# Moving a bank subtraction and a norm's sum behind the first group's sums on VectorE, in a matmul with RMSNorm

## The chip, the cores and the metric

The kernel runs on one core of one Trainium2 chip. The metric is the device time of one execution in microseconds (us). The program gives each engine its own list of instructions: TensorE (PE in the profile) multiplies, PEld is its weight load, VectorE is DVE, ScalarE is ACT, GpSimd is POOL, SyncE is SP. This kernel's matmuls write into eight banks of the memory called PSUM; a bank can be given to a new product only when the last reader of the old one is done with it.

## The reference

```python
# a: 2048x2048, b: 2048x2048, gamma: 2048, all float32; eps = 1e-5
x = np.matmul(a, b)
rms = np.sqrt(np.mean(x ** 2, axis=-1, keepdims=True) + eps)
return gamma * x / rms
```

## The kernel before

A is cut into 16 blocks of 128 rows. Blocks 0 to 3 are the "head". The others are worked in "groups" of two blocks, group 2 (blocks 4 and 5) first. Within a group, each half of the columns is computed by seven products (of eight matmuls each) rather than eight, at the price of sums: VectorE makes the sums s1, s2, s5, s6, s7 of quarters of the transposed A, and it and ScalarE combine the seven results. (In the code below, `...` marks what was cut, and the comments are added.)

```python
def take_transposed(mb, g, view, copy):            # half a transposed block: PSUM -> at(mb)
    copy(out=at(mb)[:, g * 8:(g + 1) * 8, :], in_=view)

def row_norm(mb):                                  # ScalarE: norm of a row of A, for scaling to fp16
    ... # two Squares with an accumulator (L219), then:
    nc.scalar.activation(out=norm[mb], in_=n2[:, 0:1], func=ACTF.Sqrt, ...)          # L222

def row_factor(mb):                                # VectorE: needs norm[mb]
    ...
    nc.vector.tensor_scalar_max(out=s, in0=norm.pop(mb), scalar1=1e-18)              # L227
    ...

def a_sums(g, which, lo=0, hi=KP):                 # VectorE: s1, s2, ... of a group       L260
    a11, a12, a21, a22 = (quarter(g, r, c) for r in range(2) for c in range(2))
    terms = {1: (a11, a22, ALU.add), 2: (a21, a22, ALU.add), 5: (a11, a12, ALU.add), ...}
    ...

def take_rms(mb):                                  # the norm of a row of the output
    ...
    nc.vector.reduce_sum(out=tot, in_=msq.pop(mb), axis=...)                         # L335
    ...
    nc.scalar.activation(out=rms_of[mb], in_=tot, func=ACTF.Sqrt)                    # L337
```

The boundary between the head and the groups; the change is made here:

```python
p6 = new_bank()
product(PAIR, 1, 6, p6)                            # TensorE: last product of the head
a_sums(G0, (5,))                                   # needs block 4 only
nc.vector.tensor_tensor(out=x22, in0=pair[1], in1=x22, op=ALU.subtract)   # L551, reads a bank
for g in range(2):
    turn(HB + 1, g)                                # TensorE transposes half of block 5
    take_transposed(HB + 1, g, turned[HB + 1, g], nc.vector.tensor_copy)  # L192
square_half(0, 1)
square_half(1, 1)
take_rms(0)
a_sums(G0, (2, 1))                                 # need block 5
```

The first half of group 2 (j=0), written out in order of issue (`p2`, `p5` and the others are PSUM banks; seven rotate in a pool, and the eighth, `tbank`, last served a transpose). A hook is work of other blocks that is put between the products:

```python
# hook 0: finish(0, (1,))
product(g, j, 5, p5)                               # group 2, j=0: product 5 is first
nc.scalar.copy(out=c, in_=p5)                      # L591
# hook 1: row_norm(6); take_rms(1)
product(g, j, 2, p2)
nc.vector.tensor_tensor(out=t, in0=p2, in1=c, op=ALU.add)                 # L595
# hook 2: row_factor(6); finish(0, (0,)); row_apply(6); row_norm(7); a_sums(2, (7, 6));
#         finish(1); row_factor(7); pair_sums(); pair_ends()
product(g, j, 1, p1)
nc.vector.tensor_tensor(out=t, in0=p1, in1=t, op=ALU.subtract)            # L599
product(g, j, 4, p2, start=False)                  # accumulates into p2: waits for L595
...                                                # products 3, 7, 6; then j=1: 2, 5, 1, 4, 3, 7, 6

def pair_ends():
    nc.vector.tensor_tensor(out=x11, in0=p7, in1=x11, op=ALU.add)   # L565: frees the head's p7 bank
    nc.vector.tensor_tensor(out=x22, in0=p6, in1=x22, op=ALU.add)   # L566
```

In the built program, p5 of the second half (j=1) of group 2 is given the PSUM bank that L565 frees. That is not visible in the source; it follows from the order in which banks are taken and released.

Of the kernel before, what the change touches and what calls it, by code (L numbers as in the profile page):

```python
# [13 lines left out]
ALU = mybir.AluOpType  # L14
# [3 lines left out]
def kernel(  # L18
# [13 lines left out]
    nc = tc.nc  # L32
# [12 lines left out]
    G0 = HB // 2  # L45
# [200 lines left out]
    def quarter(g, r, c):  # L246
        if g < G0:
            return head_at[:, c::2, 2 * g + r, :]
        return at(2 * g + r)[:, c::2, :]

    def sum_of(g, s):
        return s_sum[s].bitcast(BF16) if g < G0 else s_sum[s]

    def a_sums(g, which, lo=0, hi=KP):
        a11, a12, a21, a22 = (quarter(g, r, c) for r in range(2) for c in range(2))
        terms = {1: (a11, a22, ALU.add), 2: (a21, a22, ALU.add), 5: (a11, a12, ALU.add),
                 6: (a21, a11, ALU.subtract), 7: (a12, a22, ALU.subtract)}
        for s in which:
            x, y, op = terms[s]
            nc.vector.tensor_tensor(out=sum_of(g, s)[:, lo:hi, :], in0=x[:, lo:hi, :],  # L260
                                    in1=y[:, lo:hi, :], op=op)
# [44 lines left out]
    def square_half(mb, h):  # L306
        c = n_sq[mb]
        n_sq[mb] += 1
        sq = sq_pool.tile([P, 2 * CH], BF16, name="sq")
        nc.scalar.activation(out=sq, in_=x_tile(mb, h), func=ACTF.Square,  # L310
                             scale=inv_sqrt_n, accum_out=msq[mb][:, c:c + 1])

    def x_tile(mb, h):


        if (mb, h) not in x_half:
            n = n_x[0]
            n_x[0] += 1
            if n < 8:
                slot = n  # L320
            else:
                g = n // 4
                slot = ((0, 4, 1, 5), (0, 1, 4, 5))[g // 2 % 2 == 0][n % 4] + 2 * (g % 2)
            x_half[mb, h] = x_slot[slot]
        return x_half[mb, h]

    def x_chunk(mb, c):
        return x_tile(mb, c // 2)[:, (c % 2) * CH:(c % 2 + 1) * CH]
# [3 lines left out]
    def take_rms(mb):  # L332

        tot = stat_pool.tile([P, 1], FP32, name="tot")
        nc.vector.reduce_sum(out=tot, in_=msq.pop(mb), axis=mybir.AxisListType.X)  # L335
        rms_of[mb] = stat_pool.tile([P, 1], FP32, name="rms")
        nc.scalar.activation(out=rms_of[mb], in_=tot, func=ACTF.Sqrt)  # L337
# [123 lines left out]
    pair = {}  # L461
# [57 lines left out]
    x11, x12, x21, x22 = (x_chunk(r, c) for r in (r2, r3) for c in (2, 3))  # L519
# [28 lines left out]
    p6 = new_bank()  # L548
    product(PAIR, 1, 6, p6)
    a_sums(G0, (5,))  # L550
    nc.vector.tensor_tensor(out=x22, in0=pair[1], in1=x22, op=ALU.subtract)  # L551
    for g in range(2):
        turn(HB + 1, g)
        take_transposed(HB + 1, g, turned[HB + 1, g], nc.vector.tensor_copy)
    square_half(0, 1)
    square_half(1, 1)
    take_rms(0)
    a_sums(G0, (2, 1))

    def pair_sums():  # L560
        nc.vector.tensor_tensor(out=x11, in0=x22, in1=x21, op=ALU.add)
# [284 lines left out]
```

## Time and profile before

| | before |
|---|---|
| time, 3 runs | 221.41 us (221.40 to 221.79) |
| span of the profiled run | 219.9 us |
| PE busy | 209.3 us (95%) |
| VectorE, ScalarE busy | 165.9 us (75%), 127.0 us (58%) |

TensorE is the limit. Its listed waits in the kernel before are four, of which three end before 12 us; the fourth (waiter, what it waited for, us in total, times, longest us) is:

```profile
PE acc L285 <- DVE s L260: 0.5, 1, 0.5
```

That one wait, for VectorE's sums, is the last before a long unbroken run. The end of the chain of waits (start us, us, what) shows it:

```profile
68.60 0.67 DVE s L260
69.27 0.05 issue
69.32 141.76 PE acc L285 x656
```

From 69.32 us, TensorE issues 656 matmuls and waits for nothing. So time won ahead of 69.32 us is won for the whole kernel, provided that nothing inside the run becomes late. The timeline of TensorE in the kernel before (start us, us, engine, line, operation, tiles and shapes, count, and in brackets the idle time before with what ended it):

```profile
66.97 1.89 PE L285 MATMUL acc<-b,s 128*128 128x512 bf16 x8
69.32 1.90 PE L285 MATMUL acc<-b,s 128*128 128x512 bf16 x8 [0.46 <-DVE s L260]
71.06 1.89 PE L285 MATMUL acc<-t_left,s 128*128 128x512 bf16 x8
72.78 3.62 PE L285 MATMUL acc<-t_left,at_even 128*128 128x512 bf16 x16
76.24 7.07 PE L285 MATMUL acc<-b,s 128*128 128x512 bf16 x32
83.14 1.89 PE L285 MATMUL acc<-early,s 128*128 128x512 bf16 x8
...
210.92 1.91 PE L790 MATMUL acc<-b,s 128*128 128x256 bf16 x16
```

These are product 5; 2; 1; 4 and 3; 7 and 6 followed by 2 and 5 of the second half; and 1 of the second half; the last line is the two half-size products at the very end. The pitch of two matmuls is read from the starts, 3.46 us for 16, thus 0.216 us; the 0.379 us that a matmul is given in the records contains a modelled end. Product 2 could have started at 66.97 + 8 x 0.216 = 68.70 us and started at 69.32, so 0.62 us of issue time were lost, not the 0.46 us in the bracket.

VectorE at the same place (timeline, kernel before), from s5 to the instruction that frees the bank:

```profile
66.05 0.69 DVE L260 TENSOR_TENSOR s<-at_even 128x1024 f16<-128x1024 f16 x1 [0.21 <-ACT at_even L192]
66.66 0.68 DVE L551 TENSOR_TENSOR x<-acc,x 128x512 f32<-128x512 f32 x1
67.26 0.68 DVE L192 COPY at_even<-tbank 128x1024 f16<-128x1024 f16 x1
67.86 0.68 DVE L192 COPY at_even<-acc 128x1024 f16<-128x1024 f16 x1
68.46 0.14 DVE L335 TENSOR_REDUCE tot<-msq 128x1 f32<-128x5 f32 x1
68.57 1.29 DVE L260 TENSOR_TENSOR s<-at_even 128x1024 f16<-128x1024 f16 x2
...
72.07 0.15 DVE L227 TENSOR_SCALAR s<-norm 128x1 f32<-128x1 f32 x1
...
79.78 0.68 DVE L565 TENSOR_TENSOR x<-acc,x 128x512 f32<-128x512 f32 x1
```

And ScalarE (timeline, kernel before): the square root of the norm's sum, the copy behind it, and the root that ends the row norm of block 6.

```profile
68.64 0.20 ACT L337 ACTIVATE rms<-tot 128x1 f32<-128x1 f32 x1
68.89 0.59 ACT L591 COPY head_at<-acc 128x512 f32<-128x512 f32 x1
...
71.74 0.29 ACT L222 ACTIVATE norm<-n 128x1 f32<-128x1 f32 x1
```

The three views together hold what follows. The subtraction (L551) and the norm's sum (L335) stand ahead of the sum s2 for which TensorE waits. But ScalarE's root L337 starts as soon as L335 has ended, the copy L591 and the row norm up to L222 follow behind it, and VectorE's L227 starts 0.04 us after L222's end. And L565 ends at 80.46 us, while TensorE wants its bank at 83.14 - 1.73 = 81.41 us: 0.95 us of slack, about 0.9 us after the 0.05 us that a release takes to reach TensorE (s2 ended at 69.27 in the chain above, and product 2 started at 69.32).

### The profile page before, as it was taken

How to read it: one execution, taken by the hardware profiler on the slowest of the kernel's cores; microseconds unless marked ns; L12 is line 12 of the kernel's file. 1: busy time of each engine (PE TensorE's matmuls, PEld its weight loads, DVE VectorE, ACT ScalarE, POOL GpSimd, SP SyncE). 2: the span in 40 equal slices, each digit the busy share in tenths (PEclk: the TensorE clock that was granted, in tenths of full speed). 3: DMA queues.
4: the chain of work that ended last, by engine and by line, in shares of the span. 5: the costliest groups of instructions: out<-in, count | busy, mean ns of one | idle time of the engine just before them, and what ended most of it. 6: DMA issues, size and time to landing. Idle time of an engine off the chain costs nothing.

```text
span 219.9 us, 3044 instructions
## 1 busy us (share of the span) xinstructions
PE 209.3 (95%) x1032; PEld 97.4 (44%) x1032; DVE 165.9 (75%) x326; ACT 127.0 (58%) x263; POOL 36.3 (16%) x75
## 2 busy tenths in 40 slices
PE   7799999999999999999999999999999999999970
PEld 3344544444454444444444444444444444444440
DVE  1128799999889999979795639946695659787781
ACT  2110002920599898688745997289747996334471
POOL 7544443343020002100200002000200000000040
PEclk9999999999999999999999999999999999999996
DMA  7999999999929895948799049965699249145045
GB/s 157 164 203 206 199 206 208 212 206 228 409 76 362 291 293 118 358 176 230 213 300 405 3 93 265 351 247 95 156 294 405 42 100 364 73 174 210 1 171 212
DMA packets 36864, 46.60 MB, mean 212 GB/s; under 512 B 22256, under 2 KB 26352, under 8 KB 35568
## 3 DMA queue, kind: packets, MB, share of 16 engines
q0 software_dynamic: 10608, 23.86, 44.1%
q1 hardware_dynamic: 25824, 22.02, 33.5%
q10 hardware_dynamic: 416, 0.52, 0.7%
q8 instruction: 8, 0.13, 0.2%
q14 instruction: 8, 0.07, 0.1%
HBM read 34.60 MB, written 16.78 MB: 234 GB/s over the span
## 4 chain that ended last, share of the span: by engine, by line
PE 65%; DMA 23%; ACT 4%; POOL 2%; issue 1%; DVE 1%; ACTq 0%; POOLq 0%
PE acc L285 64%; DMA b<-in_b_dram 14%; DMA early<-in_a_dram 5%; DMA a<-in_a_dram 4%; ACT sq L219 2%; POOL b L102 1%; ACT at_even L192 1%; PE acc L790 1%; POOL early L106 1%; DVE s L260 1%; DVE at_even L192 0%; ACT x L729 0%; DVE x L551 0%; ACT norm L222 0%; ACT x L531 0%
## 5 line engine op out<-in xcount | busy, mean ns | idle before, releaser
L285 PE MATMUL acc<-b,s 128*128 128x512 bf16 x408 | 93.3, 379 | 0.5 <-DVE s L260 0.5
L285 PEld LDWEIGHTS <-s 128*128 128x128 f16 (+1 forms) x512 | 49.9, 98 | 60.4 <-DVE s L260 1.0
L388 PE MATMUL acc<-b,head_at 128*128 128x512 bf16 x176 | 43.2, 379 | 1.2 <-DMA b<-in_b_dram 1.2
L303 ACT ACTIVATE sq<-x 128x512 bf16<-128x512 f32 x53 | 33.4, 630 | 6.9 <-DVE x L722 3.0
L370 DVE SCALAR_TENSOR_TENSOR x<-x,r,gamma_sb 128x1024 f32<-128x1024 f32 x28 | 34.8, 1282 | 0.7
L219 ACT ACTIVATE sq<-a 128x1024 bf16<-128x1024 f32 x24 | 25.3, 1053 | 2.1 <-DMA a<-in_a_dram 1.5
L388 PEld LDWEIGHTS <-head_at 128*128 128x128 bf16 x176 | 16.9, 98 | 20.6 <-issue 1.6
L242 ACT ACTIVATE head_at<-a,s 128x2048 f16<-128x2048 f32 x10 | 20.0, 1998 | 3.3 <-DVE s L229 3.3
L102 POOL DMA_DIRECT2D b<-in_b_dram x32 | 17.2, 540 | 20.8 <-DMA b<-in_b_dram 15.0
L430 ACT COPY x<-acc 128x512 f32<-128x512 f32 x5 | 2.9, 582 | 24.7 <-PE acc L388 24.7
L285 PEld LDWEIGHTS <-head_at 128*128 128x128 f16 (+1 forms) x112 | 10.9, 98 | 13.2
L285 PE MATMUL acc<-early,head_at 128*128 128x512 bf16 x64 | 14.5, 379 | 0.0
L285 PEld LDWEIGHTS <-at_even 128*128 128x128 f16 x96 | 9.4, 98 | 11.3
L285 PE MATMUL acc<-early,s 128*128 128x512 bf16 x56 | 14.2, 379 | 0.0
L260 DVE TENSOR_TENSOR s<-head_at 128x1024 f16<-128x1024 f16 (+5 forms) x22 | 13.4, 635 | 0.1
L609 DVE TENSOR_TENSOR x<-x,x 128x512 f32<-128x512 f32 x9 | 6.2, 692 | 8.8 <-ACT x L607 8.3
L127 POOL COPY pace<-x 128x1 f32<-128x1 f32 x4 | 1.7, 413 | 66.7 <-DVE x L618 65.6
L591 ACT COPY x<-acc 128x512 f32<-128x512 f32 x9 | 5.2, 573 | 11.5 <-PE acc L285 11.5
L173 DVE COPY head_at<-tbank 128x1024 bf16<-128x1024 bf16 x7 | 4.8, 692 | 8.7 <-PE tbank L168 8.5
L285 PE MATMUL acc<-t_left,s 128*128 128x512 bf16 x48 | 11.3, 379 | 0.0
L774 POOL TENSOR_SCALAR x<-x,r 128x512 f32<-128x512 f32 x1 | 2.7, 2652 | 51.2 <-DVE r L346 51.2
L276 DVE TENSOR_TENSOR b<-b 128x1024 bf16<-128x1024 bf16 x16 | 10.8, 684 | 0.2
(113 smaller groups left out, 237.5 us busy)
## 6 DMA issues: line engine op xcount, KB each, us to landing
out_dram<-x SPq DMA_DIRECT2D x29, 512.0 KB, 3.8
a<-in_a_dram POOLq DMA_DIRECT2D x10, 1024.0 KB, 8.7
b<-in_b_dram POOLq DMA_DIRECT2D x32, 256.0 KB, 10.0
a<-in_a_dram POOLq DMA_DIRECT2D x4, 512.0 KB, 9.8
early<-in_a_dram POOLq DMA_DIRECT2D x7, 256.0 KB, 10.2
gamma_sb<-in_gamma_dram POOLq DMA_DIRECT2D x2, 512.0 KB, 8.3
out_dram<-x SPq DMA_DIRECT2D x3, 256.0 KB, 2.6
out_dram<-a SPq DMA_DIRECT2D x1, 512.0 KB, 3.3
```

The source lines that it names most:

```text
L102: nc.gpsimd.dma_start(out=raw[j][kp][:, t, :], in_=b[lo:lo + P, j * HALF:(j + 1) * HALF])
L173: nc.vector.tensor_copy(out=head_at[:, 2 * kp:2 * kp + 2, :, :], in_=view)
L219: nc.scalar.activation(out=junk, in_=a32[mb][:, h * HALF:(h + 1) * HALF], func=ACTF.Square, scale=2.0 ** -8, accum_out=n2[:, h:h + 1])
L242: nc.scalar.activation(out=a16[mb], in_=a32.pop(mb), func=ACTF.Copy, scale=factor.pop(mb))
L260: nc.vector.tensor_tensor(out=sum_of(g, s)[:, lo:hi, :], in0=x[:, lo:hi, :], in1=y[:, lo:hi, :], op=op)
L276: nc.vector.tensor_tensor(out=flat[:, 1:3, :], in0=flat[:, 1:3, :], in1=flat[:, 0::3, :], op=ALU.add)
L285: nc.tensor.matmul(bank, lhsT[:, kp, :], rhs, start=(start and kp == 0), stop=(kp == KP - 1), skip_group_check=not start)
L303: nc.scalar.activation(out=sq[:, 0:CH], in_=src, func=ACTF.Square, scale=inv_sqrt_n, accum_out=msq[mb][:, c:c + 1])
L370: nc.vector.scalar_tensor_tensor(out=x, in0=x, scalar=inverse_of[mb], in1=gamma_sb[:, h * HALF:(h + 1) * HALF], op0=ALU.mult, op1=ALU.mult)
L388: nc.tensor.matmul(bank, head_at[:, kt, r, :], head_rhs(c, kt), start=(kt == 0), stop=(kt == KT - 1))
L591: nc.scalar.copy(out=c, in_=one[1])
L609: nc.vector.tensor_tensor(out=t, in0=t, in1=x12, op=ALU.add)
```

## The change

The intent is that VectorE does first what TensorE waits for: the copies of block 5's transposes and the sums s2 and s1, then the bank's subtraction and the norm's sum.

```diff
     a_sums(G0, (5,))
-    nc.vector.tensor_tensor(out=x22, in0=pair[1], in1=x22, op=ALU.subtract)
     for g in range(2):
         turn(HB + 1, g)
         take_transposed(HB + 1, g, turned[HB + 1, g], nc.vector.tensor_copy)
     square_half(0, 1)
     square_half(1, 1)
+    a_sums(G0, (2, 1))
+    nc.vector.tensor_tensor(out=x22, in0=pair[1], in1=x22, op=ALU.subtract)
     take_rms(0)
-    a_sums(G0, (2, 1))
```

The order on the other engines is the same in the two built programs. One side effect: the banks of products 7 and 6 of group 2 are swapped, because pair[1]'s bank is released later.

## The prediction

> **What bounds it.** TensorE. The page gives PE busy for 209.3 of 219.9 us, and the chain of waits that ended last is one unbroken run of 656 matmuls from 69.32 us to the end. It starts at the boundary that this change touches: the waits give TensorE one 0.46 us wait for VectorE's first-group sums (L260). The timeline shows it: group 2's first product starts at 66.97 us; eight matmuls at a pitch of 0.216 us end at 68.70, but the second product starts only at 69.32, because its sum s2 ends at 69.26. So 0.62 us of issue time is lost there (the view counts a matmul's modelled end, hence 0.46).
>
> **What the change moves.** Nothing is added or removed; the order on the other engines is unchanged. On VectorE the bank subtraction (0.68 us, pitch 0.60) and the norm's sum (0.15) go from before s2 to behind s2 and s1.
>
> **Gain.** The first copy can start once the transposes end (66.68), at about 66.72, not 67.26; the second at 67.32; s2 at 68.05, ending 68.73; TensorE goes on at about 68.79 instead of 69.32: 0.53 us won.
>
> **Price.** The norm's sum ended at 68.60; it now ends behind s2, s1 and the subtraction, at about 70.00. ScalarE's square root waits for it (68.64 before, about 70.03 now) with everything later behind it: the Trainium skill, "PSUM — Partial Sum Buffer", section "Engine vs sequencer instructions", calls the ScalarE and VectorE queues strict FIFO, and the trace agrees (L337 at 68.64, L591 at 68.89, L219 at 69.38, back to back). So the next block's row norm ends at 73.4 instead of 72.03. VectorE reached L227, which needs that norm, at 72.02, with no slack; it now waits until about 73.46, and all behind it comes 1.39 us later:
> - s7 ends at about 76.05 (74.66 before). TensorE, 0.53 us earlier, wants it at 75.71: about 0.4 us of the gain is lost.
> - L565, which frees the head's p7 bank for p5 of the second half of group 2, ended at 80.46; TensorE wanted that bank at 81.41. It will end at about 81.85: TensorE stalls and starts that product at about 81.9, some 0.5 us later than before.
>
> After that, slack of over a microsecond at each bank and sum should absorb the shift, so the rest keeps this 0.5 us.
>
> **Predicted time.** 221.4 + 0.5 = 221.9 us, range 221.2 to 222.5 (low end: VectorE catches up; high end: another late bank, or the loads of A, which also come later). Faster by over 2%: 0.005; within 2%: 0.985; slower: 0.01.
>
> **What the profile would show.**
> 1. TensorE's s2 product starts near 68.8 (the L260 wait there is nearly gone).
> 2. ScalarE idles about 1.3 us before the square root L337, released by VectorE's L335, which starts near 69.85.
> 3. VectorE idles about 1 us before L227, released by ScalarE's L222.
> 4. TensorE waits about 0.2 us (modelled) before product 7 for L260, and about 0.5 us near 81.9 for L565.
> 5. The run of matmuls then continues without gaps, about 0.5 us later than before; the tail is unchanged.
>
> **What would make it wrong.** If the norm's delay were shorter than I think, or L227 had slack, L565 would be in time and the gain of 0.1 to 0.5 us would stay (220.9 to 221.3). If a later load or bank is also late, it is slower still. Run-to-run spread (221.40 to 221.79) is nearly as large as the effect.

## The result, and the profile after

The changed kernel took 222.10 us (median of 6 runs, 221.87 to 222.46), the kernel before 221.59 us (6 runs, 221.40 to 221.86). The ratio is 1.0023 with a 95% interval of 1.001 to 1.0036: slower by a quarter of a per cent, which by the 2% measure is the same. A ratio here is the mean time of one kernel's runs over that of the other's runs of the same rounds, so it is not quite the ratio of the medians. Executions over 1.5% slower than the fastest of the same kernel are left out of the means.

The waits of TensorE in the changed kernel no longer name the sums. In their place:

```profile
PE acc L285 <- DVE x L565: 0.5, 1, 0.5
```

The end of the chain of waits, changed kernel: the unbroken run starts later now, and behind L565.

```profile
80.54 0.69 DVE x L562
81.24 0.61 DVE x L565
81.89 129.66 PE acc L285 x600
```

TensorE's timeline, changed kernel:

```profile
67.11 3.73 PE L285 MATMUL acc<-b,s 128*128 128x512 bf16 x16
70.67 1.89 PE L285 MATMUL acc<-t_left,s 128*128 128x512 bf16 x8
72.61 3.61 PE L285 MATMUL acc<-t_left,at_even 128*128 128x512 bf16 x16
76.08 5.35 PE L285 MATMUL acc<-b,s 128*128 128x512 bf16 x24
81.89 1.89 PE L285 MATMUL acc<-b,s 128*128 128x512 bf16 x8 [0.46 <-DVE x L565]
83.61 1.89 PE L285 MATMUL acc<-early,s 128*128 128x512 bf16 x8
...
211.39 1.91 PE L790 MATMUL acc<-b,s 128*128 128x256 bf16 x16
```

Products 5 and 2 are now one stretch of 16, so the hole ahead of product 2 has all but gone: product 1 starts 3.56 us after product 5, against 3.45 us (16 pitches) without any hole and 4.09 us before. But two other holes have come. Product 4 starts at 72.61 instead of 70.67 + 1.73 = 72.40 us, and product 5 of the second half at 81.89 instead of 76.08 + 24 x 0.216 = 81.26 us. The first has no bracket, because 0.21 us is hardly more than what the modelled end hides.

VectorE, changed kernel:

```profile
66.86 0.69 DVE L192 COPY at_even<-tbank 128x1024 f16<-128x1024 f16 x1 [0.20 <-PE tbank L185]
67.47 0.68 DVE L192 COPY at_even<-acc 128x1024 f16<-128x1024 f16 x1
68.18 1.29 DVE L260 TENSOR_TENSOR s<-at_even 128x1024 f16<-128x1024 f16 x2
69.40 0.68 DVE L557 TENSOR_TENSOR x<-acc,x 128x512 f32<-128x512 f32 x1
70.00 0.15 DVE L335 TENSOR_REDUCE tot<-msq 128x1 f32<-128x5 f32 x1
...
71.88 0.68 DVE L595 TENSOR_TENSOR t_first<-acc,head_at 128x512 f32<-128x512 f32 x1
73.44 0.15 DVE L227 TENSOR_SCALAR s<-norm 128x1 f32<-128x1 f32 x1 [0.88 <-ACT norm L222]
...
81.15 0.68 DVE L565 TENSOR_TENSOR x<-acc,x 128x512 f32<-128x512 f32 x1
```

ScalarE, changed kernel:

```profile
70.18 0.20 ACT L337 ACTIVATE rms<-tot 128x1 f32<-128x1 f32 x1 [1.52 <-DVE tot L335]
70.28 0.57 ACT L591 COPY head_at<-acc 128x512 f32<-128x512 f32 x1
...
73.11 0.29 ACT L222 ACTIVATE norm<-n 128x1 f32<-128x1 f32 x1
```

Read from top to bottom, this is a chain. L335 starts 1.54 us later than before; ScalarE stands idle 1.52 us for it, with everything else queued behind; its row norm L222 starts 1.37 us later; VectorE idles 0.88 us for that norm, and L227 starts 1.37 us later; L565 starts 1.37 us later, 7.71 us after L227 as before; and 1.37 us is more than the 0.9 us of slack that the bank had. (L335's 1.54 us shrink to 1.37 on the way because L591 follows L337 after 0.10 us here and after 0.25 us before; e4 below shows what L591 waited for in the kernel before.) The same root also holds VectorE directly: the reciprocal L346, which needs it, starts at 70.41 us after 0.27 us of idle time, and so L595 comes 0.55 us later than before.

The sum for the stretch in which TensorE works on group 2 and all that follows, from the first matmul of product 5 to the first of the two half-size products at the very end (L790): 210.92 - 66.97 = 143.95 us before, and 211.39 - 67.11 = 144.28 us after. The hole ahead of product 2 shrank from 0.62 to 0.10 us (0.52 won), and 0.21 + 0.63 us came in (0.84 lost); 0.32 is the difference, next to 0.33 measured. The difference of 0.33 us is less than the 0.5 us between the medians; the section "Why the prediction was right" comes back to this. This "product stretch" is used below, because it is free of two things that the change doesn't touch and that differ from run to run: when the head ends (here 67.11 against 66.97), and how long the last store takes.

### The profile page after: what moved, and what is told of

It is laid out like the page before. It is cut to its first block, busy times and chain, and to the rows that moved or that the text cites. A ratio compares the mean times of both kernels' runs of the same rounds, so it can differ in the third digit from the quotient of the medians.

```text
span 220.3 us, 3044 instructions
## 1 busy us (share of the span) xinstructions
PE 209.8 (95%) x1032; PEld 97.7 (44%) x1032; DVE 165.9 (75%) x326; ACT 126.8 (58%) x263; POOL 36.3 (16%) x75
## 4 chain that ended last, share of the span: by engine, by line
PE 85%; DVE 5%; DMA 3%; ACT 2%; issue 1%; POOL 1%; ACTq 0%; POOLq 0%
PE acc L285 64%; PE acc L388 16%; DMA early<-in_a_dram 3%; PE tbank L419 2%; DVE x L370 2%; PE tbank L168 2%; ACT sq L219 1%; DVE s L260 1%; PE acc L790 1%; DVE at_even L192 1%; POOL b L102 0%; PE tbank L185 0%; ACT x L729 0%; DVE head_at L173 0%; DVE x L562 0%
## 5 line engine op out<-in xcount | busy, mean ns | idle before, releaser
L591 ACT COPY x<-acc 128x512 f32<-128x512 f32 x9 | 5.2, 573 | 11.5 <-PE acc L285 11.5
```

What stands on the lines that cost most here:

```text
L591: nc.scalar.copy(out=c, in_=one[1])
```

## The experiments

The theory: the later norm's sum holds up ScalarE, ScalarE holds up VectorE's L227, and L565 then frees a bank too late. The rivals: the later subtraction itself or the swap of two banks that it brings; later loads of A, which follow from the same delay; or noise. Eight kernels were run in two calls; the second call was on another chip. The chip of the first call was restless (runs of before from 221.53 to 224.46 us), so its time intervals are wide.

| kernel | norm's sum L335 starts | L565 starts | L565, from product 5's start | product stretch | ratio to before [95%] |
|---|---|---|---|---|---|
| before | 68.46 | 79.78 | 12.81 | 143.95 | 1 |
| the change | 70.00 | 81.15 | 14.04 | 144.28 | 1.0023 [1.0010, 1.0036] |
| e1 norm first, subtraction last | 67.92 | 79.78 | 12.82 | 143.42 | 0.9970 [0.9934, 1.0006] |
| e8 the same on another chip | 67.90 | 79.77 | 12.83 | 143.43 | 0.9986 [0.9971, 1.0000] |
| e2 only the norm late | 69.81 | 80.98 | 14.03 | 144.26 | 1.0021 [0.9984, 1.0057] |
| e3 change, eighth bank | 69.96 | 81.13, not waited for | 14.05 | 143.76 | 0.9994 [0.9958, 1.0030] |
| e4 before, eighth bank | 68.11 | 79.75, not waited for | 12.82 | 143.64 | 1.0011 [0.9968, 1.0055] |
| e5 norm half as late | 68.78 | 79.94 | 13.03 | 143.60 | 1.0001 [0.9987, 1.0014] |
| e6 norm later still | 70.26 | 81.43 | 14.52 | 144.76 | 1.0048 [1.0034, 1.0061] |
| e7 e1 with s2 in halves | 67.93 | 79.79 | 12.82 | 143.46 | 0.9998 [0.9978, 1.0018] |

(Times in us, from one profile each; only the change, e2 and e6 wait for L565. In e3 and e4 the added line moves L591 and L595 to L592 and L596. In e5, e6 and e7 the added lines move L565 to L566, L566 and L567, and in e5 and e6 L591 and L595 to L592 and L596.)

### e1: the norm's sum first, the subtraction last

```diff
 # against the change
+    take_rms(0)
     a_sums(G0, (2, 1))
     nc.vector.tensor_tensor(out=x22, in0=pair[1], in1=x22, op=ALU.subtract)
-    take_rms(0)
```

> Only the subtraction moves behind the sums; the norm's sum stays ahead of them (it fits in the 0.1 us in which s2 waits for the second copy anyway). Theory (late norm sum, then ScalarE, then VectorE's L227, then L565 and the bank): square root L337 at about 68.6 as in the kernel before, L227 near 72.1 to 72.2, L565 near 79.9, no TensorE wait after 69 us, s2 product near 68.8; 0.45 to 0.5 us faster than before, 0.9 to 1.0 faster than the change. Rival (the later subtraction, or the swap of the two PSUM banks that goes with it, costs the time): no faster than the change, ratio to before about 1.002.

The median was 221.75 us against 222.16 us; the interval of the ratio includes 1. The trace shows the square root at 68.61, L227 at 72.06, L565 at 79.78, and TensorE without any wait after the head. TensorE's timeline of e1 (a count of 15 or 31 is a matmul whose record is missing):

```profile
66.96 3.73 PE L285 MATMUL acc<-b,s 128*128 128x512 bf16 x15
70.52 1.89 PE L285 MATMUL acc<-t_left,s 128*128 128x512 bf16 x8
72.25 3.62 PE L285 MATMUL acc<-t_left,at_even 128*128 128x512 bf16 x16
75.70 7.07 PE L285 MATMUL acc<-b,s 128*128 128x512 bf16 x31
```

From 70.52 us on, each start follows the last by its number of pitches. The hole is gone and no new one has come: 0.53 us shorter than before and 0.86 us shorter than the change. The subtraction is as late as in the change and the banks are swapped as in the change, so neither of these costs the time. Keeping the norm's sum ahead costs nothing: s2 starts 0.71 us after the second copy in e1 (67.32 to 68.03), where the sum stands between them, and 0.71 us in the change (67.47 to 68.18), where it doesn't; so s2 waits that long in any case, by its times for the copy. VectorE's timeline of e1:

```profile
67.32 0.68 DVE L192 COPY at_even<-acc 128x1024 f16<-128x1024 f16 x1
67.92 0.15 DVE L335 TENSOR_REDUCE tot<-msq 128x1 f32<-128x5 f32 x1
68.03 1.29 DVE L260 TENSOR_TENSOR s<-at_even 128x1024 f16<-128x1024 f16 x2
```

### e2: only the norm's sum moved

```diff
 # against before
-    take_rms(0)
     a_sums(G0, (2, 1))
+    take_rms(0)
```

> The kernel before with only the norm's sum moved behind s2 and s1; subtraction and PSUM banks as before. Theory: s2 product at 69.3 as before, L337 near 69.95 (1.3 us later), L565 about 1.3 us later and TensorE stalled 0.4 us for it: 0.4 us slower than before (ratio about 1.002). Rival (subtraction or banks): same as before.

The median was 222.58 against 222.16 us; the interval of the ratio includes 1. The trace of this run is as the theory has it: product 2 at 69.34 us, L337 at 69.99, L565 at 80.98, and TensorE starting product 5 of the second half at 83.44 - 1.73 = 81.71 us, behind L565's end at 81.66. Its product stretch is 0.31 us longer than before (I had said 0.4), with the subtraction and the banks left alone. In ScalarE's timeline of e2 the idle time is there again:

```profile
69.99 0.20 ACT L337 ACTIVATE rms<-tot 128x1 f32<-128x1 f32 x1 [1.23 <-DVE tot L335]
```

### e3 and e4: another bank for product 5 of the second half

```diff
 # e3 against the change; e4 is the same edit against before
-        p2, p5 = new_bank(), new_bank()
+        p2 = new_bank()
+        p5 = ps_t.tile([P, CH], FP32, name="tbank") if (g, j) == (G0, 1) else new_bank()
```

> The changed kernel, but p5 of the second half of group 2 takes the PSUM bank that the transposes have left idle instead of the bank that L565 frees. Norm, ScalarE, VectorE and the loads of A are as late as in the changed kernel. Theory: the wait for L565 at 81.9 disappears, TensorE starts that product about 0.6 us earlier; a small new wait (0.1 us) possibly for L595 two products on: 0.5 us faster than the change, level with before (ratio 0.999 to 1.001). Rival (later loads of A or busier queues slow the rest): as slow as the change.

> Control: the same other bank in the kernel before, where the bank came free 0.9 us before it was wanted. Theory: same time as before (ratio 0.9995 to 1.0005). If it is faster by 0.3 us or more, the other bank helps for another reason than L565.

In e3, ScalarE and VectorE are as late as in the change (L337 at 70.15, L227 at 73.41, L565 at 81.13), but TensorE does not wait for L565 any more. TensorE's timeline of e3:

```profile
76.06 5.35 PE L285 MATMUL acc<-b,s 128*128 128x512 bf16 x23
81.25 1.89 PE L285 MATMUL tbank<-b,s 128*128 128x512 bf16 x8
```

81.25 us is 24 pitches after 76.06 us. The hole of 0.63 us is gone, and the product stretch is 0.52 us shorter than the change's: a new hole of about 0.07 us ahead of product 3 (it starts at 86.50, and L596, the L595 of the others, which it needs, ends at 86.45) takes some of it back, as expected. So the late loads of A, which e3 still has (the first load of A after the boundary is issued at 86.83 us, against 86.79 in the change and 85.53 in before), do not make the change slow; the bank does. In time the two kernels were level with before (222.22 and 222.34 against 222.16 us), which on that chip says little: e3's span was 220.4 us although its TensorE finished earlier than the change's, since its last stores took 3.9 and 4.1 us to land instead of 3.3 and 3.5.

e4 was to show no gain, and by time it shows none, with a wide interval. But its product stretch is 0.31 us shorter than that of before, more than the 0.3 us at which I had said the bank would help for another reason. The cause is not the bank: the shorter stretch is there already at product 2, which starts 2.05 us after product 5 in e4 and 2.35 us after it in before. VectorE's s5 started at 65.70 us in e4 and 66.05 in before, at nearly the same place of TensorE (66.93 and 66.97). The code of the two up to there is the same, so this is spread of the head. It means that the hole that the change aims at is not 0.62 us in each execution; in e4 it was 68.98 - 66.93 - 1.73 = 0.32 us. TensorE's line of product 2 in e4, and ScalarE's of the copy behind the root L337:

```profile
68.98 1.90 PE L285 MATMUL acc<-b,s 128*128 128x512 bf16 x8 [0.15 <-DVE s L260]
68.86 0.59 ACT L592 COPY head_at<-acc 128x512 f32<-128x512 f32 x1 [0.37 <-PE acc L285]
```

The second line shows something that the reading of before had missed. The norm's sum was 0.35 us earlier here, and the root L337 too (68.29 us), but the copy was not: it waited 0.37 us for product 5. In all five kernels with the sum ahead of s2 (before, e1, e4, e7, e8) this copy starts 1.92 or 1.93 us after product 5 does, and L565 12.81 to 12.83 us after it. So a sum that is a little late is at first absorbed here: 0.37 us in e4, some 0.15 us in before.

### e5 and e6: half the delay, and more of it

```diff
 # e5 against before
-    take_rms(0)
-    a_sums(G0, (2, 1))
+    a_sums(G0, (2,))
+    take_rms(0)
+    a_sums(G0, (1,))

 # e6 against the change
     nc.vector.tensor_tensor(out=x22, in0=pair[1], in1=x22, op=ALU.subtract)
+    nc.vector.tensor_copy(out=spare[1], in_=x22)
     take_rms(0)
```

> Half the dose: the kernel before with the norm's sum between s2 and s1, so about 0.6 to 0.7 us late instead of 1.3. Theory: L565 and the bank come 0.7 us later, which is inside the 0.9 us by which the bank was early; no TensorE wait for L565, product stretch from group 2's first matmul to the last two half products 143.9 to 144.0 us as before, time as before (ratio 0.999 to 1.001). Rival (every late norm costs in proportion): about 0.2 to 0.25 us slower.

> A larger dose: the changed kernel with one more copy of 128x512 floats on VectorE (into a tile that is overwritten later) ahead of the norm's sum, so that the sum comes another D = 0.4 to 0.8 us later. Theory: beyond the slack each further delay costs in full: TensorE waits for L595 before its fourth product and for L565 before p5 of the second half, each D longer after the other; total D slower than the change, 0.4 to 0.8 us. Rival (the change costs through something other than the norm's delay): as the change, 144.3 us of product stretch.

e5 took 221.61 us against 221.44 us, ratio 1.0001 (0.9987 to 1.0014). TensorE did not wait for the bank: VectorE freed it at 80.62 us and TensorE took it at 82.74 - 1.73 = 81.01 us. The stretch was shorter than I had said (143.60 us), because this run too had the small hole at the boundary (0.29 us), as e4 had: VectorE's s5 started at 65.65 us, 1.26 us ahead of product 5 instead of 0.92. For the same reason only 0.22 us of the slack was used and not 0.7, so the run does not refute the rival as sharply as it was meant to; e6 does (at the rate of e2, 0.31 us for a delay of 1.22, a further 0.48 us would have cost 0.12). e6 took 222.54 us, ratio 1.0048. Counted from product 5's start, L335 came 0.46 us later in e6 than in the change, L565 0.48 us later, and the stretch was 0.48 us longer. TensorE's timeline of e6 names both waits:

```profile
72.88 3.61 PE L285 MATMUL acc<-t_left,at_even 128*128 128x512 bf16 x16 [0.52 <-DVE t_first L596]
76.36 5.35 PE L285 MATMUL acc<-b,s 128*128 128x512 bf16 x23
82.17 1.89 PE L285 MATMUL acc<-b,s 128*128 128x512 bf16 x8 [0.46 <-DVE x L566]
```

The first of them is the hole ahead of product 4 that has no bracket in the change: product 4 accumulates into the bank that L595 (L596 here) must have read. The three kernels that wait for the bank (the change, e2, e6) agree in one number: stretch less L565's start in the table is 144.28 - 14.04 = 130.24, 144.26 - 14.03 = 130.23 and 144.76 - 14.52 = 130.24 us. There TensorE starts its remaining run when L565 lets it, and holes won or lost ahead of L565 make no difference. In before, L565 at 12.81 would allow a stretch of 143.05 us; it was 143.95, so L565 was early by 0.90 us. This is the slack, and e5, with a delay of 0.22 us and no wait, and e2, with 1.22 us and a wait, lie on either side of it.

### e7 and e8: the better version once more

```diff
 # e7 against e1 (e8 is e1 unchanged)
-    a_sums(G0, (2, 1))
+    a_sums(G0, (2,), 0, KP // 2)
+    a_sums(G0, (2,), KP // 2, KP)
+    a_sums(G0, (1,))
```

> The version with the norm's sum first and the subtraction last, with s2 made in two halves, the first of which needs only the first copy. Theory: the 0.1 us that TensorE still waits for s2 goes; product stretch about 143.3 us instead of 143.42; in time at most 0.1 us better than the version without the split, 0.5 to 0.7 us faster than before, not to be told from it by timing.

> The same kernel as e1_norm_first on this call's chip, because the runs of before spread by over 1 us on the last one: 0.4 to 0.6 us faster than before (ratio about 0.9975), product stretch 143.4 us, no TensorE wait after 66 us.

e8 took 221.15 against 221.44 us, ratio 0.9986 (0.9971 to 1.0000), with a stretch of 143.43 us. The gain is 0.3 us and not the 0.4 to 0.6 us I had expected; on the other chip it was 0.4 us by medians. A cause that fits, but was not separated, is the spread of the hole in before: 0.62 us in its one profile, and 0.66, 0.32 and 0.29 us in e2, e4 and e5, which have the same code up to s2. In these four, the hole and the time by which s5 starts ahead of product 5 (0.92, 0.88, 1.23 and 1.26 us) add up to 1.54 or 1.55 us, so this lead sets the hole. Neither s5 nor product 5 needs anything that the change moves; over the ten profiles this lead is 1.08 us in the mean (0.88 to 1.26), which gives, as an estimate, a mean hole of 0.46 us in before and a gain of 0.36 us for e1. e7 did close the last 0.1 us at the boundary (product 1 follows product 5 by 3.45 us, 16 pitches), but 0.15 us came in at 108.56 us, where product 4 of group 3's second half by its times waited for ScalarE's L593 (the L591 of the others), which ended at 108.50 us; in e8 the same copy ended at 108.04 and was in time. Its time misses the 0.5 to 0.7 us that I had expected: 221.21 against 221.44 us, ratio 0.9998. With one of its six runs at 222.39 us that is inconclusive, and e1 is the version to keep.

## Why the prediction was right

The predicted 221.9 us (221.2 to 222.5) stands against 222.10 us, and the predicted 0.5 us against 0.51 us by medians. The mechanism was right; that the size agrees to 0.01 us is luck. The interval of the ratio allows 0.2 to 0.8 us, and the two profiles show only 0.33 us. Two errors of the prediction offset each other. It let L565 end at 81.85, so start 81.17 - 66.97 = 14.20 us after product 5, where the trace has 14.04, because it had not seen that 0.15 us would be made up at L591; this made its loss 0.16 us too large. And it took the hole of the one profile of before, 0.62 us, for the usual one, where the estimate from ten profiles (under e8) is 0.46; this made its gain 0.16 us too large. With the smaller hole, before would have a stretch of 143.79 us and the change, at 144.28, would be 0.49 us longer; this too is an estimate.

- What bounds the kernel, and the gain: right. The hole ahead of product 2 shrank by 0.52 us, predicted 0.53.
- The price on ScalarE: right. Its idle time was 1.52 us (predicted 1.3), since the norm's sum started at 70.00 us instead of 69.85: the first copy waited for the transposes until 66.86 us, not 66.72, because TensorE was 0.14 us later in this run; the rest is that ScalarE was done with its squares 0.08 us earlier. L337 came at 70.18 (predicted 70.03), L222's end at 73.40 (predicted 73.4): L591 had made up the 0.15 us.
- The price on VectorE: right. L227 came at 73.44 (predicted 73.46), after 0.88 us of idle time (predicted about 1).
- The first new wait: the wrong place. I had put 0.4 us ahead of product 7, for s7. The trace has 0.21 us ahead of product 4, for L595, and next to nothing ahead of product 7: s7 ended at 76.03 us and product 7 started at 76.08, just where TensorE, already held up, arrived. My own numbers would have told this. With the root L337 at 70.03 us, ending at 70.23, L595 would start some 1.6 us later (the reciprocal L346 and L595 lie 71.33 - 69.78 = 1.55 us apart in before), so at about 71.8, and end at about 72.5; product 4 was wanted at 68.79 + 2 x 1.73 = 72.25 us. The prediction does not mention L595. It cost the prediction nothing, because the wait at L565 takes the time of whatever came before it.
- The second new wait: right. L565 ended at 81.83 (predicted about 81.85), and the product started at 81.89 (predicted about 81.9). The view gave it 0.46 us (predicted about 0.5).
- That nothing is late afterwards: right. From 83.14 us before, and from 83.61 us after, to the first matmul of L790, the time is 127.78 us in both (210.92 - 83.14 and 211.39 - 83.61).

The Trainium skill, "PSUM — Partial Sum Buffer", section "Engine vs sequencer instructions", on which the prediction rested, calls the ScalarE and VectorE queues strict FIFO. All traces here agree: in the change, L591 needed a product that was finished at about 69 us and had to wait behind L337 until 70.28 us.

That the chain starts at the norm's sum is shown by e1 (norm back, subtraction late: no loss), e2 (norm late alone: the loss) and e5 and e6 (the dose); that its last link is the bank is shown by e3. The links between, from ScalarE's queue to L227 and L565, are read from the traces, in which each is late by the same 1.37 us; no experiment cut one of them alone. That the swap of banks and the later loads of A cost nothing is shown by e1 and e3. What stays open is why s5's lead over product 5 differs from run to run, and the exact gain of e1: 0.3 and 0.4 us by medians, with intervals that touch or include 1, next to the estimate of 0.36.

## What to carry to other kernels

Before moving an instruction behind the ones that the limiting engine waits for, follow what the moved instruction itself releases: a 0.15 us sum on VectorE was the head of ScalarE's queue, and through it and a PSUM bank it held up TensorE 11 us later. Compare each later link's slack with the delay, in absolute times from the trace; a delay within the slack is free (e5, with 0.22 us), and beyond it costs in full (e6). And do not take the hole of one profile for the usual one. Last, move only what gains: the small sum fitted free of charge into the 0.1 us in which the next sum waits for the copy, and only the subtraction, with 0.60 us of VectorE's time, was worth moving (e1, by its trace; by time its gain is not clear of noise).

## What the Trainium skill lacked or had wrong

- "Perfetto Trace Analysis", section "Tensor Engine Instruction (MATMUL, LD_WEIGHTS)", says that a matmul's end is estimated by the profiler; the traces agree. It does not say that this hides waits: with 0.379 us recorded for a matmul and a pitch of 0.216 us, a hole of 0.62 us was shown as 0.46, and one of 0.21 us ahead of product 4 was shown as none.
- "VectorE: DVE Perf Modes", section "The DRAIN you can't avoid", says that in its chain of copies a semaphore after each costs nothing extra. Here, a sum that needs the result of the copy just ahead of it starts 0.71 us after that copy, where an instruction that doesn't need the copy's result starts 0.60 us after it (L192 to L335, 67.86 to 68.46, in the kernel before). A 0.15 us sum put between the two was free (e1). The page does not say whether its copies need one another's results, so this is a case that it lacks and not one that it has wrong.
- No page that I looked at says that an execution's engines can meet at a boundary with an offset that differs from run to run: with the same code up to there, the hole at the boundary was 0.62, 0.66, 0.32 and 0.29 us in the profiles of before, e2, e4 and e5. One profile's hole is not the mean gain.
